# Order of the first query/key unit, and a passage into the feed-forward whose sums run on VectorE

## The chip, the cores and the metric

The kernel runs on one core of a Trainium2 chip. The metric is the device time of one execution in microseconds (us), read as the median of several executions.

## What is computed

One layer of a hybrid encoder, on 1024 tokens of width 1024 in float32. The input is RMS-normalised and projected; half of the heads do differential attention, the other half an mLSTM; both go through one output projection, then a gated feed-forward (SwiGLU) of hidden width 2816 and a last RMS norm follow. Cut to what matters here:

```
h = rms_norm(x, mix_norm_g);  z = h @ w_in
da_q, da_k, da_v, ml_q, ml_k, ml_v, ml_o, ml_i, ml_f = split(z)
x = x + concat(diff_attention(...), mlstm(...)) @ w_out
h2 = rms_norm(x, ffn_norm_g)
x = x + (silu(h2 @ w_gate) * (h2 @ w_up)) @ w_down
return rms_norm(x, final_norm_g)
```

## The kernel before, in words

**Numbers.** Every float32 matrix product is three matmuls on a high and a low part: `split` (L106) casts a tile to its high part on ScalarE (L107) and subtracts for the low part on VectorE (L108), or on GpSimd if the call names it. `mul12` (L182) is twelve 128x128 by 128x512 matmuls (L186 to L188) into one PSUM bank.

**Units.** The query/key projection and the feed-forward's gate and up projections use a 2x2 block scheme with seven products. `unit` (L193) works on one block of weights (`st`, four 128x512 tiles a11, a12, a21, a22) and on seven prepared operands: b11, b21, b22 (blocks of the activations) and t1 to t4 (their sums and differences). Its steps are numbered 1 to 7, each one `mul12`, and a sequence gives their order. Steps 1 and 2 add into bank 0, 5 and 3 into bank 3, 7 and 4 into bank 2, 6 into bank 1. Step 1 copies bank 0 into `u2` (ScalarE, L212), and step 2 then adds its product into the same bank. After step 6, `u2` takes bank 1 (L220); after step 7, c22 = u2 + bank 2 + bank 3 (L224, L225), and step 4 then adds into bank 2 (c21, L231). `SEQ0` is (1, 2, 5, 6, 7, 4, 3) and `SEQ` is (1, 5, 6, 7, 2, 4, 3); `SEQ0` is used by the first query/key unit and by the two first feed-forward units, `SEQ` by all others. A unit's split weights go through a ring of five (later seven) tiles.

**The first stage.** Eight query/key units run one after the other (L655 on). While the first one runs, ScalarE still finishes the output gate of the mLSTM (tanh, L534), the split of t4, and the first tables. `late_start` puts four of the tanh and t4 behind the cast of the first unit's fourth step.

**The passage.** The output projection (`out_proj`, L1099) goes row block by row block (128 tokens); for each it adds the residual (L1149, called the x add below), squares on ScalarE (L1169), takes the root on GpSimd (L1170, L102), scales on VectorE (`h2`, L1173), and later transposes `h2` (`h2_out`, L1071). The last four rows are the second half of the tokens, in the order given by `SLICES`. For each of them `t_slices` (L1054) makes one slice of t1, t3 and b22, and `t_sums` (L1065) adds two sums into `hst`, from which t2 and t4 are made. Of this, GpSimd does the low parts and the sums of the first two slices (`TP` = 2), two of the four low parts of b21 (`B21` = 2), and the low parts of t4; VectorE the rest. After the last row of the output projection TensorE runs step 1 of both first feed-forward units, then the eight transposes of the last row's `h2` (`th2l`), then the other steps of the two units by turns.

**Order.** TensorE's order is written by hand in the first stage and in the passage. The order of the instructions on the other engines, and on TensorE during attention, comes from a list scheduler that has its own clock; `tc.issue_after(i)` holds an instruction in that order behind `i`. All engines but the DMA work in the order of their queues.

Of the kernel before, what the change touches and what calls it, by code (L numbers as in the profile page):

```python
# [34 lines left out]
TP = 2  # L35
B21 = 2
# [8 lines left out]
SEQ0 = (1, 2, 5, 6, 7, 4, 3)  # L45
SEQ_D = (1, 5, 2, 3, 6, 7, 4)
# [16 lines left out]
def block_kernel(ctx, tc, x, xT, pos, cols, gate_b, lam_in, w_vg, w_mo, w_qk, w_dv,  # L63
# [42 lines left out]
    def split(hi, lo, src, eng=None):  # L106
        last_cast[0] = act.copy(hi, src)  # L107
        last_cast[1] = (eng or dve).tensor_sub(lo, src, hi.bitcast(F32))  # L108

# [83 lines left out]
    def unit(st, h, seq, psg, ringc, tmp, done, low=None):  # L193
# [13 lines left out]
        u2 = c22 = c21 = None  # L207
        for step in seq:
# [8 lines left out]
            elif step == 6:  # L217
                dve.tensor_tensor(a21, a22, a11, op=ALU.subtract)
                mul12(bank(1), wsplit(a21), h["t2"], True)
                dve.tensor_add(u2, u2, bk[1])  # L220
            elif step == 7:
                mul12(bank(2), wsplit(a11), h["t3"], True)
                c22 = tmp("u3")
                dve.tensor_add(c22, u2, bk[2])  # L224
                dve.tensor_add(c22, c22, bk[3])  # L225
            elif step == 2:
                mul12(bk[0], wsplit(a12), h["b21"], False)
            elif step == 4:
                mul12(bk[2], wsplit(a22), h["t4"], False)
                c21 = tmp("c21")  # L230
                dve.tensor_add(c21, u2, bk[2])  # L231
                if low:
                    low((c21, c22))
            elif step == 3:
                dve.tensor_tensor(a21, a12, a21, op=ALU.subtract)
                mul12(bk[3], wsplit(a21), h["b22"], False)
                dve.tensor_add(u2, u2, bk[3])
# [150 lines left out]
    with ExitStack() as pa:  # L388
# [3 lines left out]
        with ExitStack() as pm:  # L392
# [262 lines left out]
            for n_, b in enumerate(UO):  # L655
# [4 lines left out]
                u_ = q_unit(b, st, SEQ if n_ else SEQ0)  # L660
# [393 lines left out]
    def t_slices(c):  # L1054
        cs = slice(c * P, (c + 1) * P)
        p1, p2 = b12[:, :, cs], b22[:, :, cs]
        tt = bw.tile([P, 4, P], F32, tag="tt", name="tt", bufs=1)
        dve.tensor_sub(tt, p1, hst[0][:, :, cs])
        eng = pool if c in SLICES[:TP] else dve
        split(H["t1"][0][:, :, cs], H["t1"][1][:, :, cs], tt, eng)  # L1060
        dve.tensor_sub(p1, p2, p1)
        split(H["t3"][0][:, :, cs], H["t3"][1][:, :, cs], p1, eng)
        split(H["b22"][0][:, :, cs], H["b22"][1][:, :, cs], p2, eng)

    def t_sums(c):  # L1065
        cs = slice(c * P, (c + 1) * P)
        eng = pool if c in SLICES[:TP] else dve
        eng.tensor_tensor(hst[0][:, :, cs], hst[0][:, :, cs], b12[:, :, cs], op=ALU.add)
        eng.tensor_tensor(hst[1][:, :, cs], hst[1][:, :, cs], hst[0][:, :, cs], op=ALU.subtract)

    def h2_out(i, h2, ps_tile, gs=(0, 1)):  # L1071
# [16 lines left out]
        if i >= 4 and 1 in gs:  # L1088
            if hst:
                t_slices(i - 4)  # L1090
# [5 lines left out]

    n_wo = []

    def out_proj():  # L1099
# [29 lines left out]
        while True:  # L1129
# [5 lines left out]
            for u in range(2):  # L1135
# [4 lines left out]
                for n_, k in enumerate((4, 5, 6, 7, 0, 1, 2, 3)):  # L1140
# [9 lines left out]
                    if prev and 8 * u + n_ in th[2:]:  # L1150
                        g = th[2:].index(8 * u + n_)
                        h2_out(*prev, d_tile, (g,))
                        if g:
                            prev = None
                            if i == LAST:
                                t_sums(SLICES[2])
                    yield
                if u == 0 and i == LAST:
                    for n, g in (("b11", 0), ("b21", 1)):
                        H[n] = [slots.tile([P, 4, 512], F32R, tag=f"A{hl}{g}", name=n) for hl in range(2)]  # L1160
                        for q in range(4):
                            split(H[n][0][:, q], H[n][1][:, q], hst[g][:, q], pool if g and q < B21 else dve)
                    for c in SLICES[:2]:
                        t_sums(c)
            ssq = bw.tile([P, 1], F32, tag="ssq2", name="ssq2")
            sp.dma_start(x1_d[i], x1)
            with tc.high_priority():
# [5 lines left out]
                dve.tensor_scalar_mul(h2, x1, rs)  # L1173
            prev = (i, h2)
            if i == LAST:
                out_last.append(prev)
# [76 lines left out]
    two = [gu_unit(0, m, SEQ0) for m in range(2)]  # L1253
# [8 lines left out]
    for _ in range(2):  # L1262
        for u in two:
            next(u)
    t_sums(SLICES[3])
    for n, g in (("t2", 0), ("t4", 1)):
        H[n] = [slots.tile([P, 4, 512], F32R, tag=f"B{hl}{g}", name=n) for hl in range(2)]
        for q in range(4):
            split(H[n][0][:, q], H[n][1][:, q], hst[g][:, q], pool if g else dve)
# [13 lines left out]
    for _ in range(len(SEQ0)):  # L1283
        for u in two:
            next(u, None)
# [250 lines left out]
```

## Time and profile before

| what | value |
|---|---|
| median of 3 runs | 1218.44 us (1218.09 to 1219.29) |
| the profiled execution's own time | 1217.11 us |
| its span, first to last instruction | 1215.3 us |
| TensorE busy in the span | 1179.6 us (97%) |
| VectorE busy | 874.8 us (72%) |
| ScalarE busy | 526.3 us (43%) |
| GpSimd busy | 145.0 us (12%) |
| mean granted TensorE clock | 0.991 |

The profiled execution lies 1.3 us under the median of the runs, and 1.8 us of it lie outside its span. Engines: PE is TensorE, DVE VectorE, ACT ScalarE, POOL GpSimd, SP the queue that issues most DMAs.

### The profile page before, as it was taken

What the parts mean: (1) busy time and instruction counts of PE and PEld (TensorE: products, weight loads), DVE (VectorE), ACT (ScalarE), POOL (GpSimd) and SP (SyncE); (2) the same over time, 40 slices, a digit from 0 to 9 for tenths busy, and PEclk for the clock granted to TensorE, in tenths of its full rate; (3) what the DMA queues carried; (4) which work ended last, traced back from release to release, by engine and by line L of the source; (5) the groups of instructions that cost most, each with busy time, mean ns of one, the idle gap of its engine ahead of it and who ended that gap; (6) DMA issues with size and microseconds to landing.
All of it is one profiled execution on the core that took longest, in us unless ns stands there. A gap on an engine that the chain in (4) does not pass through costs nothing.

```text
span 1215.3 us, 15877 instructions
## 1 busy us (share of the span) xinstructions
PE 1179.6 (97%) x5692; PEld 973.4 (80%) x5692; DVE 874.8 (72%) x1520; ACT 526.3 (43%) x1111; POOL 145.0 (12%) x125
## 2 busy tenths in 40 slices
PE   9899999899989999998999999999999999999997
PEld 7678888898877888876888888888888888888885
DVE  8768899566768766659766766667666779765674
ACT  6723354335666555546333223332333245444552
POOL 0100000120101100043301110111101111000000
PEclk9999999999999999999999999999999999999999
DMA  9467743700667442150323230322223269733241
GB/s 332 167 170 192 219 128 123 258 19 19 215 224 229 149 139 95 57 221 18 113 87 130 95 130 36 130 109 117 79 87 130 96 242 352 259 99 112 79 149 70
DMA packets 87487, 172.37 MB, mean 142 GB/s; under 512 B 9968, under 2 KB 42864, under 8 KB 81008
## 3 DMA queue, kind: packets, MB, share of 16 engines
q1 hardware_dynamic: 85656, 169.73, 40.8%
q10 hardware_dynamic: 1752, 1.62, 0.4%
q8 instruction: 45, 0.74, 0.3%
q14 instruction: 34, 0.28, 0.1%
HBM read 117.58 MB, written 53.74 MB: 141 GB/s over the span
## 4 chain that ended last, share of the span: by engine, by line
PE 86%; DMA 2%; issue 2%; DVE 2%; ACT 2%; POOL 1%; SPq 0%; ACTq 0%; POOLq 0%; DVEq 0%
PE g L186 16%; PE g L187 16%; PE g L188 16%; PE y L1453 6%; PE y L1452 6%; PE y L1454 6%; PE dwo L1145 2%; PE dwo L1143 2%; PE dwo L1144 2%; PE to L333 2%; PE s L290 1%; PE s L291 1%; PE ddv L143 1%; PE ddv L142 1%; PE ddv L144 1%
## 5 line engine op out<-in xcount | busy, mean ns | idle before, releaser
L107 ACT CAST w<-st 128x512 fp32r<-128x512 f32 x218 | 133.4, 620 | 292.6 <-PE g L188 158.1
L108 DVE TENSOR_TENSOR w<-st,w 128x512 fp32r<-128x512 f32 x218 | 159.2, 733 | 91.7 <-ACT w L107 90.3
L186 PE MATMUL g<-t,w 128*128 128x512 f32 x448 | 177.9, 397 | 0.0
L187 PE MATMUL g<-t,w 128*128 128x512 f32 x448 | 177.1, 395 | 0.0
L188 PE MATMUL g<-t,w 128*128 128x512 f32 x448 | 176.4, 394 | 0.0
L1453 PE MATMUL y<-fhl,w 128*128 128x512 f32 x308 | 122.1, 397 | 0.0
L1452 PE MATMUL y<-fhl,w 128*128 128x512 f32 x308 | 121.8, 395 | 0.0
L1454 PE MATMUL y<-fhl,w 128*128 128x512 f32 x308 | 120.9, 393 | 0.0
L187 PE MATMUL g<-b,w 128*128 128x512 f32 x264 | 104.9, 397 | 0.0
L186 PE MATMUL g<-b,w 128*128 128x512 f32 x264 | 104.2, 395 | 0.0
L188 PE MATMUL g<-b,w 128*128 128x512 f32 x264 | 104.0, 394 | 0.0
L186 PEld LDWEIGHTS g<-t,w 128*128 128x128 f32 x448 | 84.2, 188 | 22.4 <-DVE u L224 2.6
L188 PEld LDWEIGHTS g<-t,w 128*128 128x128 f32 x448 | 84.2, 188 | 20.1
L187 PEld LDWEIGHTS g<-t,w 128*128 128x128 f32 x448 | 84.3, 188 | 19.0
L107 ACT CAST w<-gs 128x512 fp32r<-128x512 f32 x76 | 46.5, 619 | 68.7 <-PE y L1454 51.6
L108 DVE TENSOR_TENSOR w<-gs,w 128x512 fp32r<-128x512 f32 x76 | 52.9, 703 | 28.8 <-ACT w L107 28.8
L108 DVE TENSOR_TENSOR fhl<-w,fhl 128x512 fp32r<-128x512 f32 x77 | 51.9, 710 | 26.2 <-ACT fhl L107 26.2
L1452 PEld LDWEIGHTS y<-fhl,w 128*128 128x128 f32 x308 | 57.8, 188 | 14.2
L1454 PEld LDWEIGHTS y<-fhl,w 128*128 128x128 f32 x308 | 57.9, 188 | 13.8
L1453 PEld LDWEIGHTS y<-fhl,w 128*128 128x128 f32 x308 | 58.0, 188 | 13.1
L107 ACT CAST fhl<-w 128x512 fp32r<-128x512 f32 x77 | 44.2, 618 | 46.7 <-PE y L1454 43.3
L1237 POOL TENSOR_TENSOR ss<-sg 128x512 f32<-128x512 f32 x11 | 17.3, 1569 | 354.2 <-DVE sg L1235 317.9
(342 smaller groups left out, 2539.2 us busy)
## 6 DMA issues: line engine op xcount, KB each, us to landing
st<-in_w_gu SPq DMA_DIRECT2D x22, 1024.0 KB
gs<-gm_d SPq DMA_DIRECT2D x76, 256.0 KB
gm_d<-sg SPq DMA_DIRECT2D x11, 1024.0 KB
w<-in_w_dn SPq DMA_DIRECT2D x44, 256.0 KB
gm_d<-ss SPq DMA_DIRECT2D x11, 768.0 KB
st<-in_w_qk SPq DMA_DIRECT2D x8, 1024.0 KB
qbuf<-q_d SPq DMA_DIRECT2D x64, 128.0 KB
q_d<-xt SPq DMA_DIRECT2D x24, 256.0 KB
```

Of the source, the lines that this page charges most:

```text
L107: last_cast[0] = act.copy(hi, src)
L108: last_cast[1] = (eng or dve).tensor_sub(lo, src, hi.bitcast(F32))
L186: pe.matmul(ps, w[0][:, ks], h[0][:, k, :], start=first and k == 0, stop=False, **sk)
L187: pe.matmul(ps, w[0][:, ks], h[1][:, k, :], start=False, stop=False, **sk)
L188: pe.matmul(ps, w[1][:, ks], h[0][:, k, :], start=False, stop=k == 3, **sk)
L333: pe.matmul(po[:, 0, :], at[:, j, :], dv[j // 4][:, j % 4, hh * P:(hh + 1) * P], start=(j == 0), stop=(j == i))
L1143: pe.matmul(ps, mh, wh, start=(n_ == 0), stop=False)
L1144: pe.matmul(ps, mh, wl, start=False, stop=False)
L1145: pe.matmul(ps, ml, wh, start=False, stop=(n_ == KC - 1))
L1452: pe.matmul(bk[q][b], gh, w[0], start=first and k == 0, stop=False, **sk)
L1453: pe.matmul(bk[q][b], gh, w[1], start=False, stop=False, **sk)
L1454: pe.matmul(bk[q][b], gl, w[0], start=False, stop=k == FH - 1, **sk)
```

## The change

Three things are changed. The first query/key unit takes the sequence of the others. The two first feed-forward units take a new sequence `SEQ1` = (1, 2, 5, 7, 6, 4, 3), in which step 7 comes before step 6, so `unit` computes c22 behind whichever of the two comes last. And in the passage all low parts and sums that GpSimd made are VectorE's now; the sums of all four slices, and the third part (b22) of the last two, are made later: held in the scheduler's order behind the low part of t3 of the last slice, as t3 of the third slice and the later steps of the two units are held behind the scaling of the last row (`scaled`).

```diff
-TP = 2
-B21 = 2
+SEQ1 = (1, 2, 5, 7, 6, 4, 3)
...
+        def c22_of():
+            nonlocal c22
+            c22 = tmp("u3")
+            dve.tensor_add(c22, u2, bk[2])
+            dve.tensor_add(c22, c22, bk[3])
...
                 dve.tensor_add(u2, u2, bk[1])
+                if 2 in bk:
+                    c22_of()
             elif step == 7:
                 mul12(bank(2), wsplit(a11), h["t3"], True)
-                c22 = tmp("u3")
-                dve.tensor_add(c22, u2, bk[2])
-                dve.tensor_add(c22, c22, bk[3])
+                if 1 in bk:
+                    c22_of()
...
-                u_ = q_unit(b, st, SEQ if n_ else SEQ0)
+                u_ = q_unit(b, st, SEQ)
...
-    def t_slices(c):
+    def t_slices(c, parts=(0, 1, 2)):
...
-        eng = pool if c in SLICES[:TP] else dve
-        split(H["t1"][0][:, :, cs], H["t1"][1][:, :, cs], tt, eng)
-        dve.tensor_sub(p1, p2, p1)
-        split(H["t3"][0][:, :, cs], H["t3"][1][:, :, cs], p1, eng)
-        split(H["b22"][0][:, :, cs], H["b22"][1][:, :, cs], p2, eng)
+        if 0 in parts:
+            tt = bw.tile([P, 4, P], F32, tag="tt", name="tt", bufs=1)
+            dve.tensor_sub(tt, p1, hst[0][:, :, cs])
+            split(H["t1"][0][:, :, cs], H["t1"][1][:, :, cs], tt)
+        if 1 in parts:
+            dve.tensor_sub(p1, p2, p1)
+            t3_in[0] = split(H["t3"][0][:, :, cs], H["t3"][1][:, :, cs], p1)
+        if 2 in parts:
+            split(H["b22"][0][:, :, cs], H["b22"][1][:, :, cs], p2)
...
-        eng = pool if c in SLICES[:TP] else dve
-        eng.tensor_tensor(hst[0][:, :, cs], hst[0][:, :, cs], b12[:, :, cs], op=ALU.add)
-        eng.tensor_tensor(hst[1][:, :, cs], hst[1][:, :, cs], hst[0][:, :, cs], op=ALU.subtract)
+        dve.tensor_add(hst[0][:, :, cs], hst[0][:, :, cs], b12[:, :, cs])
+        dve.tensor_sub(hst[1][:, :, cs], hst[1][:, :, cs], hst[0][:, :, cs])
...
-                t_slices(i - 4)
+                t_slices(i - 4, {SLICES[2]: (0,), SLICES[3]: (0, 1)}.get(i - 4, (0, 1, 2)))
...
-                            split(H[n][0][:, q], H[n][1][:, q], hst[g][:, q], pool if g and q < B21 else dve)
-                    for c in SLICES[:2]:
-                        t_sums(c)
+                            split(H[n][0][:, q], H[n][1][:, q], hst[g][:, q])
...
-                dve.tensor_scalar_mul(h2, x1, rs)
+                scaled[0] = dve.tensor_scalar_mul(h2, x1, rs)
...
+                with tc.issue_after(scaled[0].ins):
+                    t_slices(SLICES[2], (1,))
...
-    two = [gu_unit(0, m, SEQ0) for m in range(2)]
+    two = [gu_unit(0, m, SEQ1) for m in range(2)]
...
-    for _ in range(2):
+    for n in range(3):
         for u in two:
-            next(u)
-    t_sums(SLICES[3])
+            with tc.issue_after(scaled[0].ins) if n == 2 else ExitStack():
+                next(u)
+    for c in SLICES:
+        with tc.issue_after(t3_in[0].ins):
+            t_sums(c)
...
-            split(H[n][0][:, q], H[n][1][:, q], hst[g][:, q], pool if g else dve)
+            split(H[n][0][:, q], H[n][1][:, q], hst[g][:, q])
+        if g == 0:
+            for c in SLICES[2:]:
+                with tc.issue_after(t3_in[0].ins):
+                    t_slices(c, (2,))
```

How the order moves, at three places. TensorE, at the end of step 1 of the first query/key unit (`g_575` is its bank 0; `hT_126`, `hT_127` are b11, `hT_128`, `hT_129` b21, `t_531`, `t_532` t1), before:

```order
L187 MATMUL g_575<-hT_127,w 128x512
L188 MATMUL g_575<-hT_126,w 128x512
L186 MATMUL g_575<-hT_128,w 128x512
L187 MATMUL g_575<-hT_129,w 128x512
L188 MATMUL g_575<-hT_128,w 128x512
```

and in the change:

```order
L187 MATMUL g_575<-hT_127,w 128x512
L188 MATMUL g_575<-hT_126,w 128x512
L186 MATMUL g_595<-t_531,w 128x512
L187 MATMUL g_595<-t_532,w 128x512
L188 MATMUL g_595<-t_531,w 128x512
```

The second product no longer goes into bank 0: step 5 follows step 1, and b21 comes as the fifth product. ScalarE's queue at that place in the change (`og` is the gate's tanh, `t4x` the high part of t4, `u_591` the copy of bank 0):

```order
L106 CAST w<-st 128x512 x3
L542 ACTIVATE og<-po_166,rstdh 128x512
L106 CAST w<-st 128x512
L542 ACTIVATE og<-po_167,rstdh 128x512
L542 ACTIVATE og<-po_168,rstdh 128x512
L542 ACTIVATE og<-po_169,rstdh 128x512
L106 CAST t4x_647<-xx 128x512 x4
L648 ACTIVATE an<-an 128x2
L106 CAST w<-st 128x512
L219 COPY u_591<-g_575 128x512
```

The copy keeps its place at the end; one weight cast more (three here, two before) stands ahead of the gate. VectorE in the passage, around the last row's scaling (`h_5613` before, `h_5602` in the change; `x_5411` is the row's output), before:

```order
L1068 TENSOR_TENSOR hst_5256<-hst_5256,h2r_3670 128x4x128
L1149 TENSOR_TENSOR x_5411<-dwo,x_5411 128x512
L108 TENSOR_TENSOR t_5250<-h2r_3670,t_5249 128x4x128
L108 TENSOR_TENSOR w<-st,w 128x512
L1069 TENSOR_TENSOR hst_5258<-hst_5258,hst_5256 128x4x128
L218 TENSOR_TENSOR st<-st 128x512
L1173 TENSOR_SCALAR h_5613<-x_5411,rs 128x1024
```

and in the change:

```order
L1159 TENSOR_TENSOR x_5411<-dwo,x_5411 128x512
L107 TENSOR_TENSOR w<-st,w 128x512
L107 TENSOR_TENSOR t_5248<-tt,t_5247 128x4x128
L1179 TENSOR_SCALAR h_5602<-x_5411,rs 128x1024
L1070 TENSOR_TENSOR h2r_3670<-h2r_3671,h2r_3670 128x4x128
L225 TENSOR_TENSOR st<-st 128x512
L107 TENSOR_TENSOR w<-st,w 128x512
```

No sum stands ahead of the scaling any more, and two instructions instead of four stand between the x add and the scaling. GpSimd's queue in the passage keeps only the small instructions of the root; before, this stood ahead of the last of them:

```order
L108 TENSOR_TENSOR b_5552<-hst_5258,b_5551 128x512 x2
L1068 TENSOR_TENSOR hst_5256<-hst_5256,h2r_3670 128x4x128 x2
L1069 TENSOR_TENSOR hst_5258<-hst_5258,hst_5256 128x4x128 x2
L1170 TENSOR_SCALAR ssq_5611<-ssq_5611 128x1
L102 TENSOR_TENSOR rs<-ssq_5611,mhalf 128x1
L108 TENSOR_TENSOR t_5774<-hst_5258,t_5773 128x512 x4
```

The three rows of sums and low parts ahead of the root, and the four low parts of t4 behind it, are gone from that queue.

## Rows read from the trace of the kernel before

**Rows 1.** Page, part 1: busy time, share of span, instructions of each engine.
```profile
PE 1179.6 (97%) x5692; PEld 973.4 (80%) x5692; DVE 874.8 (72%) x1520; ACT 526.3 (43%) x1111; POOL 145.0 (12%) x125
```

**Rows 2.** PE's waits, whole span: line, releaser, total us, times, longest.
```profile
PE th2l L1075 <- DVE h L1173: 5.3, 1, 5.3
PE to L333 <- ACT at L326: 5.1, 6, 2.6
...
PE dvg L142 <- DVE u L237: 2.2, 1, 2.2
...
PE g L186 <- DVE uq L224: 0.8, 1, 0.8
```

**Rows 3.** Timeline of PE, first unit: start, us, instruction, [idle before <- releaser].
```profile
50.73 0.40 PE L186 MATMUL g<-hT,w 128*128 128x512 f32 x1
...
58.63 0.80 PE L186 MATMUL g<-hT,w 128*128 128x512 f32 x1 [4.95 <-ACT u L212]
...
78.27 0.39 PE L186 MATMUL g<-hT,w 128*128 128x512 f32 x1
```

**Rows 4.** Windows: us, busy (instructions) of PE, PEld, DVE, ACT, POOL, clock, DMA.
```profile
58.60:62.60 4.00, 3.97 (x9) 3.14 (x10) 0.60 (x2) 0.00 (x0) 0.00 (x0) 0.50 0.74 311
62.60:72.00 9.40, 9.22 (x40) 7.14 (x38) 5.45 (x12) 1.96 (x4) 0.00 (x0) 1.00 0.46 131
...
700.00:900.00 200.00, 200.00 (x860) 160.94 (x859) 135.09 (x184) 60.29 (x103) 29.14 (x20) 1.00 0.28 104
```

**Rows 5.** Timeline of ACT around the copy of the first unit's bank 0.
```profile
55.30 2.18 ACT L107 CAST t4x<-xx 128x512 fp32r<-128x512 f32 x4
...
57.98 0.60 ACT L212 COPY u<-g 128x512 f32<-128x512 f32 x1
```

**Rows 6.** Timeline of PE in the passage.
```profile
546.74 0.63 PE L1075 MATMUL td<-ident,h 128*128 128x128 f32 x4 [1.12 <-DVE h L1173]
547.13 0.48 PE L1143 MATMUL dwo<-wo,w 128*128 128x512 f32 x1
...
553.69 0.39 PE L1145 MATMUL dwo<-wo,w 128*128 128x512 f32 x1
...
564.97 1.97 PE L1075 MATMUL th2l<-ident,h 128*128 128x128 f32 x8 [5.31 <-DVE h L1173]
...
568.15 0.39 PE L187 MATMUL g<-b,w 128*128 128x512 f32 x1
```

**Rows 7.** Timeline of POOL in the passage.
```profile
544.68 3.05 POOL L108 TENSOR_TENSOR b<-hst,b 128x512 fp32r<-128x512 f32 x2
553.77 5.79 POOL L1068 TENSOR_TENSOR hst<-hst,h2r 128x512 f32<-128x512 f32 x2 [6.04 <-DVE b L108]
559.52 3.38 POOL L1069 TENSOR_TENSOR hst<-hst,hst 128x512 f32<-128x512 f32 x2
...
563.59 0.54 POOL L102 TENSOR_TENSOR rs<-ssq,mhalf 128x1 f32<-128x1 f32 x1
```

**Rows 8.** Timeline of DVE in the passage.
```profile
528.41 0.68 DVE L1149 TENSOR_TENSOR x<-dwo,x 128x512 f32<-128x512 f32 x1
531.28 0.75 DVE L1173 TENSOR_SCALAR h<-x,rs 128x1024 f32<-128x1024 f32 x1 [2.18 <-POOL rs L102]
...
544.82 1.78 DVE L1173 TENSOR_SCALAR h<-x,rs 128x1024 f32<-128x1024 f32 x1
...
556.62 0.68 DVE L1149 TENSOR_TENSOR x<-dwo,x 128x512 f32<-128x512 f32 x1
...
561.71 1.74 DVE L218 TENSOR_TENSOR st<-st 128x512 f32<-128x512 f32 x1
...
566.16 0.68 DVE L1081 TENSOR_TENSOR h2r<-th2l,colt 128x512 f32<-128x512 f32 x1
...
572.78 0.69 DVE L235 TENSOR_TENSOR st<-st 128x512 f32<-128x512 f32 x1
```

**Rows 9.** Windows: the passage as one stretch, columns as in rows 4.
```profile
553.00:571.00 18.00, 12.69 (x54) 10.29 (x53) 17.25 (x24) 8.16 (x18) 10.19 (x6) 0.91 0.07 29
```

More of the change, by code (lines that the diff above doesn't have):

```diff
@@ L108, in split @@
         last_cast[1] = (eng or dve).tensor_sub(lo, src, hi.bitcast(F32))
+        return last_cast[1]
     def split_scaled(hi, lo, src, scale):
@@ L1052, in block_kernel @@
     H, hst, late_c, td_pool = {}, [], [], [psd]
-    def t_slices(c):
+    def t_slices(c, parts=(0, 1, 2)):
         cs = slice(c * P, (c + 1) * P)
         p1, p2 = b12[:, :, cs], b22[:, :, cs]
-        tt = bw.tile([P, 4, P], F32, tag="tt", name="tt", bufs=1)
-        dve.tensor_sub(tt, p1, hst[0][:, :, cs])
-        eng = pool if c in SLICES[:TP] else dve
-        split(H["t1"][0][:, :, cs], H["t1"][1][:, :, cs], tt, eng)
-        dve.tensor_sub(p1, p2, p1)
-        split(H["t3"][0][:, :, cs], H["t3"][1][:, :, cs], p1, eng)
-        split(H["b22"][0][:, :, cs], H["b22"][1][:, :, cs], p2, eng)
+        if 0 in parts:
[7 more added lines that the diff above has]
+            split(H["b22"][0][:, :, cs], H["b22"][1][:, :, cs], p2)
     def t_sums(c):
         cs = slice(c * P, (c + 1) * P)
-        eng = pool if c in SLICES[:TP] else dve
-        eng.tensor_tensor(hst[0][:, :, cs], hst[0][:, :, cs], b12[:, :, cs], op=ALU.add)
-        eng.tensor_tensor(hst[1][:, :, cs], hst[1][:, :, cs], hst[0][:, :, cs], op=ALU.subtract)
+        dve.tensor_add(hst[0][:, :, cs], hst[0][:, :, cs], b12[:, :, cs])
+        dve.tensor_sub(hst[1][:, :, cs], hst[1][:, :, cs], hst[0][:, :, cs])
     def h2_out(i, h2, ps_tile, gs=(0, 1)):
@@ L1095, in d_tile @@
         return td_pool[0].tile([P, 4, P], F32, tag="d", name="td")
+    scaled, t3_in = [None], [None]
     n_wo = []
@@ L1154, in out_proj @@
                             prev = None
-                            if i == LAST:
-                                t_sums(SLICES[2])
                     yield
@@ L1282, in block_kernel @@
     raw_tiles(ssp, "12", "x12", 8, 3)
-    for _ in range(len(SEQ0)):
+    for _ in range(len(SEQ1)):
         for u in two:
-            next(u, None)
+            with tc.issue_after(scaled[0].ins):
+                next(u, None)
     for j in range(1, FH):
```

## The prediction

> **What bounds the kernel now.** I read the busy times first [rows 1]: TensorE is busy 97% of the span, VectorE 72%, GpSimd 12%. Two later views tell what that 97% is made of. In a stretch where TensorE is never idle and the granted clock is 1.00, its 860 matmuls take 200 us, 0.2326 us each [rows 4]: one of the seven steps of a unit (12 matmuls) takes 2.79 us, a unit of 84 takes 19.5. No edit of this change touches the number of matmuls, so the only time to be had is where TensorE waits or goes slower than that. The list of its waits [rows 2] names the places: 5.3 us at the last row's transposes (`th2l`), 5.1 in six waits in attention (largest 2.6), 2.2 at one wait in the first value projection (`dvg`), 0.8 for `uq`. The largest wait of the first stage is seen in the timeline: 4.95 us for the copy of bank 0 [rows 3]. Of these the change aims at the copy, `uq` and `th2l`.
>
> **First unit, what it loses now.** It begins at 50.73 and the next one at 78.27 [rows 3]: 27.5 us, against 19.5 for 84 matmuls at full pace, so 8.0 us are lost. They can be named. 4.95 is the idle time: step 2 adds into bank 0, which ScalarE copies only at 57.98 to 58.58, behind the four casts of t4 of 55.30 to 57.48 [rows 5]. Behind that idle time the granted clock is 0.50, the 1.2 GHz level, and nine matmuls take 4.0 us where the 40 behind them go at 0.235 each (9.40 by 40) at 1.00 [rows 4]: 4.0 less 9 by 0.235 is 1.9. The wait for `uq` ahead of step 4 is 0.8 [rows 2]. 0.35 is left over.
>
> **First unit, in the change.** Steps 5, 6 and 7 stand between step 1 and step 2, so TensorE asks for the copied bank at 50.73 + 4 by 2.79 = 61.9. ScalarE's queue has one more weight cast ahead of the copy (three ahead of the gate instead of two); priced by a cast of t4, a quarter of 2.18 [rows 5], that is 0.55, and the copy ends near 59.1: 2.8 us to spare, where TensorE was 4.95 late. Step 4 then asks for `c22` at 64.7. That needs step 7's bank (ready at 61.9) and two additions of about 0.6, so 63.1: step 2, which stands between them now, covers it with 1.6 to spare. b21, which step 2 reads, is only asked for later than before. t1 to t3, which are asked for earlier, are made ahead of the unit's start; their lateness would be the one thing to cost here, at most what is gained. With no idle time there is no reason for the lower clock. I take the whole **8.0**; bounds 0 (something else is late by as much) and 8.0.
>
> **Passage, what it loses now.** `th2l` waits 5.31 [rows 6]. After it, from 564.97 to 568.15, eight transposes and three matmuls take 3.18. Four transposes took 0.39 at 546.74 [rows 6], so the normal time is 2 by 0.39 + 3 by 0.2326 = 1.5; **1.7** is the slow restart. And 1.12 is the wait for the row before it (`td` at 546.74). Together 5.31 + 1.7 + 1.1 = 8.1; I take **8.0**.
> Where it comes from: the last output matmul starts at 553.69 [rows 6] and the x add that reads its bank starts at 556.62 [rows 8], 2.5 us behind its end: VectorE is in other work. From there to the scaling takes until about 564.2, because the root's last instruction runs at 563.59 [rows 7], behind four sums that kept GpSimd from 553.77 to 562.90. Undisturbed, the same chain takes 2.87 us from x add to scaling (528.41 to 531.28) and 0.75 for the scaling [rows 8]. The earlier wait has the same source: the scaling took 1.78 at 544.82 [rows 8] instead of 0.75, while GpSimd ran two low parts from 544.68 to 547.73 [rows 7].
>
> **Passage, in the change.** All times here are on the clock of the trace of before, so ahead of the 8.0 of the first stage. Without the 1.1 the last output matmul ends at 553.69 + 0.39 - 1.1 = 553.0. The x add starts by 553.3; 2.87 to the scaling, plus up to 0.6 for casts ahead of the square on ScalarE, plus 0.75: `h` is there at 556.9 to 557.6. TensorE gets to the transposes after step 1 of both units, at 564.97 - 5.31 - 1.1 = 558.6. So this wait ends, with about 1 us in hand; and without idle time the slow restart goes.
>
> **What takes its place.** VectorE gets 16 more instructions: six low parts of slices, two of b21, four sums, four low parts of t4. At normal pace VectorE does 11 of this size in 6.62 us (566.16 to 572.78 [rows 8]), 0.60 each, so **9.6 us** of work move onto an engine that was busy 17.25 of 18.0 us here [rows 9]. Against that, part of its busy time was only slowness beside GpSimd: a 128x512 subtraction took 1.74 at 561.71 while GpSimd was in its sums, against 0.68 to 0.69 [rows 8]. What matters is the first thing TensorE will be kept from. In the queue's order I count 41 VectorE instructions from the end of the scaling to the `c22` of the first of the two units, which step 4 must wait for, because it adds into the bank that `c22` reads. 557.6 + 41 by 0.60 + 0.7 for the last one's end = 582.9, if none of them waits. TensorE, after eight transposes (0.8) at 558.6, wants that step after eight steps (step 5, 7, 6 and 2 of both units): 558.6 + 0.8 + 8 by 2.79 = 581.7. So I expect a **new wait of about 1.0 us** for `c22`; bounds 0 and 3 (one more pause for t2 or a weight cast, and the slow restart behind it). The operands ahead of it are on time by the same count: t1 at 563.8 (wanted 565.0), t3 at 564.4 (wanted 570.6), t2's first part at 572.3 (wanted 576.1). GpSimd keeps the root's four small instructions alone. The weights' transfers into `st` go out when `a11` to `a22` are last read; those reads shift with TensorE, and no TensorE wait in [rows 2] is on a transfer here.
>
> **Attention.** The scheduler's clock sees other costs, and shuffles some instructions of all engines in and behind attention: the transposes of the first row stand somewhat later, the first output matmuls four places earlier. I price this at 0, with 1.5 to either side, about half of the largest wait there (2.6 [rows 2]).
>
> **Sum.** -8.0 - 8.0 + 1.0 = -15.0. The profiled execution's own time is 1217.1, so 1202.1; the median of the runs lies 1.3 above it, so **1203.5 us**.
>
> **The rivals.**
> *VectorE becomes the bound in the passage.* It is the engine with the least room there [rows 9], and takes 9.6 us more. If all of it shows (every wait of TensorE goes to VectorE's queue as soon as the root is out of the way), the sum is -16.0 + 9.6 = -6.4 and the time 1212.0. Against it: the operands' dates above, and the 1.7 us instructions that become 0.6. The Trainium skill (Perfetto Trace Analysis, Optimizing Scalar/DVE Operations) speaks against this change: with VectorE saturated, moving work to ScalarE or GpSimd may make sense. The change does the reverse; by that sentence the time would be this rival's. The same section adds that both share a port into SBUF, so that moving between those two might not help; the 1.74 beside 0.69 agrees with that part. Chance 0.15.
> *The first stage's gain is eaten later.* Units 1 to 7 and the value projection come 8 us earlier; if their weights or VectorE's rotation of q and k are already just in time, the wait at `dvg` (2.2 [rows 2]) grows by what was won. Then only the passage counts: 1218.4 - 7.0 = 1211.4. For it: `dvg` waits on VectorE already. Against: behind the first unit VectorE is busy 5.45 of 9.40 us and the DMA share is 0.46 [rows 4]. Chance 0.09.
> *Nothing comes of it*: the copy is still late, and step 1 of the passage still waits as long for another operand. Within 2.4 us of 1218.4; chance 0.05.
> *Slower.* VectorE's long instructions in the passage are not GpSimd's doing, but come with the pieces that they read. Then the pace stays near the mean of 0.60 and 1.78, 1.19 each, and 41 instructions to `c22` take 24 us longer than reckoned. Without the first 1.2 to 2 us of slack that is +25 - 16 + some 1 of restart, about 1228. The point from which it decides: 16 us by 41, a pace of 0.98 instead of 0.60. For it: the 17.25 of 18.0 for 24 instructions [rows 9], 0.72 each even as a mean. Against: the 11 in a row at 0.60 lie in the same passage [rows 8], and the 1.78 and 1.74 both fall on a time when GpSimd was busy [rows 7]. Chance 0.04.
>
> **How the numbers follow.** My forecast, with its neighbourhood (1199 to 1208: attention's 1.5 both ways, the new wait 0 to 3, a unit's operand 1 to 2 late), has 0.62; another 0.05 lies below 1199, where attention's waits go as well. The range has to take in the two middle rivals: 1199.0 to 1212.5. What can be told from no change here is 0.2%, 2.4 us. Faster by more: 0.62 + 0.05 + 0.15 + 0.09 = 0.91; the same 0.05; slower 0.04.
>
> **What will show it.** In the first unit: no wait at the second product into bank 0, granted clock 1.00 all through, the second unit starting near 70.3. In the passage: no wait at `th2l`, the scaling at most 4 us behind the x add, GpSimd all but idle, VectorE in a row at 0.60 each, and the only wait of TensorE above half a microsecond for `c22` at step 4 of the first unit. I am wrong if VectorE's instructions stay long without GpSimd, if `t1`'s slices keep TensorE waiting behind the transposes, or if the 8 us are gone by the start of attention.

## The result and the profile after

The changed kernel takes 1204.78 us (median of 4 runs, 1201.22 to 1206.66) against 1218.87 beside it: ratio 0.9882, 95% interval 0.9858 to 0.9905. That is 14.1 us; 15.0 were forecast. The profiled execution took 1204.77 us, its span is 1203.0, so it can be set against the 1217.11 and 1215.3 of before.

The page's busy times answer to [rows 1], and the list of TensorE's waits, over the whole span, to [rows 2]:

```profile
PE 1177.0 (98%) x5692; PEld 970.0 (81%) x5692; DVE 875.6 (73%) x1536; ACT 526.8 (44%) x1111; POOL 118.9 (10%) x109
```

```profile
PE to L341 <- ACT at L334: 6.9, 9, 2.6
PE dvg L142 <- DVE u L245: 2.4, 1, 2.4
PE g L186 <- DVE u L212: 1.2, 2, 0.9
```

The waits for the copy, for `uq` and for `th2l` are gone. VectorE has 16 instructions more (1536 against 1520) and all but the same busy time, 875.6 against 874.8 us: the 9.6 us that it took over are paid by instructions that no longer run at 1.7 us beside GpSimd. New are two waits for `c22` (1.2 us in all), and the waits for `at` in attention have grown from 5.1 in 6 to 6.9 in 9.

The timeline of TensorE of the changed kernel, at the places that matter (start, duration, instruction, idle time before and its releaser):

```profile
51.23 0.40 PE L186 MATMUL g<-hT,w 128*128 128x512 f32 x1
...
70.74 0.39 PE L186 MATMUL g<-hT,w 128*128 128x512 f32 x1
...
350.39 0.40 PE L144 MATMUL ddv<-w,hT 128*128 128x512 f32 x1
...
388.62 0.60 PE L1135 MATMUL td<-ident,mt 128*128 128x128 f32 x4
...
553.49 1.04 PE L1084 MATMUL th2l<-ident,h 128*128 128x128 f32 x8
...
555.28 0.40 PE L187 MATMUL g<-b,w 128*128 128x512 f32 x1
...
577.17 0.47 PE L186 MATMUL g<-t,w 128*128 128x512 f32 x1 [0.35 <-DVE u L212]
...
603.38 0.50 PE L186 MATMUL g<-t,w 128*128 128x512 f32 x1 [0.89 <-DVE u L212]
...
1195.68 0.40 PE L1470 MATMUL y<-fhl,w 128*128 128x512 f32 x1
```

Three rows of the kernel before that belong to them and are not among [rows 3] and [rows 6]:

```profile
357.86 0.40 PE L144 MATMUL ddv<-w,hT 128*128 128x512 f32 x1
...
393.83 0.60 PE L1125 MATMUL td<-ident,mt 128*128 128x128 f32 x4
...
1206.75 0.40 PE L1454 MATMUL y<-fhl,w 128*128 128x512 f32 x1
```

Put beside the same instruction in the trace of before, these give an account by stage. A shift is the start after less the start before; where no pair of rows is shown it is the median over the matmuls of 10 us.

| up to | before | after | shift | this stage |
|---|---|---|---|---|
| start of the first unit | 50.73 | 51.23 | +0.50 | +0.5 (ahead of the change) |
| start of the second unit | 78.27 | 70.74 | -7.53 | **-8.03** |
| last matmul of the last value projection | 357.86 | 350.39 | -7.47 | +0.1 |
| a `td` group in attention | 393.83 | 388.62 | -5.21 | **+2.26** |
| ahead of the passage, near 540 | | | -4.97 | +0.24 |
| second matmul group behind `th2l` | 568.15 | 555.28 | -12.87 | **-7.90** |
| behind step 4 of the two first units, near 595 | | | -12.25 | **+0.6** |
| behind step 4 of the next unit, near 620 | | | -11.09 | **+1.15** |
| last matmul | 1206.75 | 1195.68 | -11.07 | 0 |

Another 1.2 us of the 12.3 lie behind the last matmul, in the last stores: no instruction differs there. They are no gain of the change. From the start of the last matmul to the end of the span it is 8.5 us in this trace of before, and 7.3 to 7.6 in the traces of the changed kernel and of all twelve versions below.

Windows over the first unit and the passage (columns as in [rows 4]):

```profile
51.20:70.80 19.60, 19.60 (x86) 15.84 (x85) 16.34 (x32) 11.19 (x21) 0.00 (x0) 1.00 0.66 216
550.00:556.00 6.00, 6.00 (x32) 4.98 (x31) 4.97 (x9) 4.31 (x12) 0.73 (x2) 1.00 0.19 77
556.00:576.00 20.00, 20.00 (x88) 16.16 (x87) 19.81 (x34) 11.82 (x20) 0.00 (x0) 1.00 0.00 1
```

TensorE has no idle time in any of the three, and the granted clock is 1.00 where it was 0.50 behind the copy [rows 4] and 0.91 in the passage [rows 9]. The first unit takes 70.74 less 51.23, 19.51 us; 84 by 0.2326 was the forecast. ScalarE's queue there is as reckoned, the copy still behind t4 and ending at 59.61, while TensorE asks for it at 62.37:

```profile
56.33 2.19 ACT L106 CAST t4x<-xx 128x512 fp32r<-128x512 f32 x4
...
59.01 0.60 ACT L219 COPY u<-g 128x512 f32<-128x512 f32 x1
```

VectorE and GpSimd in the passage, the x add, the root and the scaling of the last row, and what stands ahead of the first `c22` (L212):

```profile
548.33 0.68 DVE L1159 TENSOR_TENSOR x<-dwo,x 128x512 f32<-128x512 f32 x1
...
551.24 0.76 DVE L1179 TENSOR_SCALAR h<-x,rs 128x1024 f32<-128x1024 f32 x1 [1.03 <-POOL rs L101]
...
575.75 0.68 DVE L107 TENSOR_TENSOR w<-st,w 128x512 fp32r<-128x512 f32 x1
576.35 0.67 DVE L212 TENSOR_TENSOR u<-u,g 128x512 f32<-128x512 f32 x1
```

```profile
550.39 0.19 POOL L1176 TENSOR_SCALAR ssq<-ssq 128x1 f32<-128x1 f32 x1 [10.66 <-ACT h L1175]
550.66 0.54 POOL L101 TENSOR_TENSOR rs<-ssq,mhalf 128x1 f32<-128x1 f32 x1
```

From x add to scaling it is 2.91 us (548.33 to 551.24); before, some 7.5 lay between them [rows 7, 8]. `h` is there at 552.0, 1.5 us ahead of the transposes. Behind it VectorE works almost without a pause: the 41st instruction, the first addition of `c22`, starts at 576.35, 40 steps of 0.61 us behind the first (551.91). TensorE comes to step 4 at 576.43 + 0.23 = 576.66 and gets its bank at 577.17, 0.51 late (the list has 0.35, since it counts from the modelled end of the matmul before).

### The profile page after: what moved, and what is told of

Same layout as the page of the kernel before. It is cut to its first block, busy times and chain, and to the rows that moved or that the text cites. A ratio compares the mean times of both kernels' runs of the same rounds, so it can differ in the third digit from the quotient of the medians.

```text
span 1203.0 us, 15867 instructions
## 1 busy us (share of the span) xinstructions
PE 1177.0 (98%) x5692; PEld 970.0 (81%) x5692; DVE 875.6 (73%) x1536; ACT 526.8 (44%) x1111; POOL 118.9 (10%) x109
## 4 chain that ended last, share of the span: by engine, by line
PE 87%; DVE 4%; DMA 3%; issue 2%; ACT 2%; SPq 1%; POOL 0%; ACTq 0%; POOLq 0%; DVEq 0%
PE g L186 15%; PE g L187 15%; PE g L188 15%; PE y L1469 6%; PE y L1468 6%; PE y L1470 6%; PE dwo L1153 2%; PE dwo L1154 2%; PE to L341 2%; PE dwo L1155 2%; PE s L298 1%; PE s L299 1%; PE po L144 1%; PE po L143 1%; PE po L142 1%
## 5 line engine op out<-in xcount | busy, mean ns | idle before, releaser
L186 PEld LDWEIGHTS g<-b,w 128*128 128x128 f32 x264 | 49.5, 188 | 12.1
```

Source lines behind the costliest of these rows:

```text
L186: pe.matmul(ps, w[0][:, ks], h[0][:, k, :], start=first and k == 0, stop=False, **sk)
```

## The experiments

All of them ask one of four things: do the two parts of the change stand for themselves, what in the passage frees the last row, what in attention costs 2.3 us, and can the new waits be had back. Ratios are to the kernel before on the same chip.

### One part alone

`e1` takes the first line of the diff alone, `e2` everything but that line.

```diff
-                u_ = q_unit(b, st, SEQ if n_ else SEQ0)
+                u_ = q_unit(b, st, SEQ)
```

> Only the first query/key unit gets the new sequence; the passage stays as before. By my account the first unit gives 8.0 us (second unit starts 8 us earlier, no wait for the copy), and the 2.3 us lost in attention between 360 and 385 us come from the same edit, because the scheduler's clock reaches attention earlier and sets another order there: time about 5.7 us under the kernel before, about 1213, and the new waits for the transposed probabilities (to) are there. Rival: attention's loss comes from the passage's edit (its instructions compete in the same scheduler); then this kernel gains the whole 8, about 1211.

> Only the passage is changed; the first unit keeps its old sequence. By my account attention is as before, the wait at the last row's transposes goes with the slow restart and the 1.1 us ahead (7.9 us), and 1.75 us come back as two waits for c22: 6 to 7 us under the kernel before, about 1212. Rival (attention's loss belongs to this edit): about 1214.5, with the new waits in attention here.

`e1`: 1210.03 us, 0.9931 (0.9905 to 0.9957). `e2`: 1209.8 us, 0.9931 (0.9907 to 0.9954). Both are faster than was expected (about 1213 and 1212), and the total of `e1` lies at its rival's 1211; so the expectations are decided by the traces, stage by stage, and not by the totals. The product of the two ratios is 0.986, the whole change 0.988: within the intervals the parts add. Of the waits of `e1`, the one at `th2l` is untouched, and the nine in attention are there:

```profile
PE to L333 <- ACT at L326: 6.9, 9, 2.6
PE th2l L1075 <- DVE h L1173: 5.3, 1, 5.3
```

In `e1` the second unit comes 8.0 us earlier, as in the changed kernel; `e2` keeps the old 5.0 us for the copy and gets the passage's -7.9, +0.6 and +1.15. The lists of the order say why the nine waits belong to `e1`: its TensorE order in attention is word for word that of the changed kernel, that of `e2` that of the kernel before. So the edit of the first unit makes the scheduler sort transposes and products in attention differently; that its own clock reaches attention at another time is the likely way, and is not shown. But `e2` lost 1.3 us in attention too, with the old order. That missed its expectation, and is taken up below.

### What frees the last row: the engine, or the place in the queue

`e3`, `e4` and `e5` leave the first unit as before. `e4` is the kernel before with VectorE in GpSimd's place and nothing held back:

```diff
-        eng = pool if c in SLICES[:TP] else dve
+        eng = dve
...
-                            split(H[n][0][:, q], H[n][1][:, q], hst[g][:, q], pool if g and q < B21 else dve)
+                            split(H[n][0][:, q], H[n][1][:, q], hst[g][:, q])
```

`e3` is `e2` with GpSimd's share of before put back, and `e5` is `e3` with its sums held behind the root (the first line of the cut is `e3`'s):

```diff
+        eng = pool if c in SLICES[:2] else dve
...
-                rsqrt_of(rs, ssq)
+                rooted[0] = rsqrt_of(rs, ssq)
...
-        with tc.issue_after(t3_in[0].ins):
+        with tc.issue_after(t3_in[0].ins), tc.issue_after(rooted[0].ins):
             t_sums(c)
```

> The passage's new order (sums and later slices held behind the scaling, step 7 before step 6) with GpSimd doing what it did before; first unit as before. If what delayed the last row's scaling was the place of the sums in GpSimd's queue, the order alone removes most of it: the scaling comes within 1 us of its time in the changed kernel and th2l waits under 1 us; GpSimd's slow sums then come later and put other waits (t2 or t4 late, each GpSimd instruction 1.7 to 2.9 us where VectorE needs 0.6): 1212 to 1218. Rival: the engine counts, since VectorE is slowed by whatever GpSimd does in the passage; then th2l still waits 2 us or more.

> All of GpSimd's sums and low parts in the passage on VectorE, but nothing held behind the scaling and the old sequence of steps; first unit as before. If the engine is what counts, th2l's wait nearly goes (under 1 us): about 1212. If the place behind the scaling counts too, VectorE's queue has up to eight more instructions of 0.6 us ahead of the x add or the scaling, and th2l still waits 1 to 4 us: 1213 to 1216.

> As the run before with GpSimd kept (first unit as before), but GpSimd's four sums now really stand behind the root's last instruction in its queue. If the sums' place in GpSimd's queue was the whole cause, the last row's scaling comes 3.5 to 4 us behind the x add and th2l waits under 0.5 us, as in the changed kernel; what remains is the 1.1 us wait one row earlier (GpSimd's two low parts beside the scaling), and afterwards the sums on GpSimd make t2 late by 0 to 4 us: 1210 to 1215. Rival: the engine counts by itself; then th2l still waits 1.5 us or more although no sum stands ahead of the root.

`e3`: 1213.17 us, 0.9966 (0.995 to 0.9982). It did not test what it was meant to. A hold binds instructions of the holder's engine alone, and the holder is VectorE's; so the four sums still stood ahead of the root on GpSimd:

```profile
553.05 3.98 POOL L1079 TENSOR_TENSOR hst<-hst,h2r 128x512 f32<-128x512 f32 x2 [6.04 <-DVE b L107]
556.99 2.52 POOL L1080 TENSOR_TENSOR hst<-hst,hst 128x512 f32<-128x512 f32 x2
559.59 0.19 POOL L1178 TENSOR_SCALAR ssq<-ssq 128x1 f32<-128x1 f32 x1
```

`th2l` waited 2.3 us, which decides neither for the expectation nor for its rival. It is less than 5.3 since VectorE, relieved of its own sums, stood idle beside them for the greater part, and GpSimd's took 2.0 and 1.3 us (means of two) instead of 2.9 and 1.7 [rows 7].

`e4`: 1214.04 us, 0.9965 (0.9953 to 0.9977), `th2l` waits 3.5 us. The sums are VectorE's and the root has GpSimd for itself, but two things hold it up. VectorE's sums stand ahead of the x add, which comes at 555.33, and then this (the row before stands above it):

```profile
543.44 0.53 POOL L1170 TENSOR_SCALAR ssq<-ssq 128x1 f32<-128x1 f32 x1 [11.78 <-ACT h L1169]
...
557.33 3.55 POOL L1170 TENSOR_SCALAR ssq<-ssq 128x1 f32<-128x1 f32 x1 [12.40 <-ACT h L1169]
560.96 0.54 POOL L102 TENSOR_TENSOR rs<-ssq,mhalf 128x1 f32<-128x1 f32 x1
```

One instruction on 128x1 takes 3.55 us on GpSimd, where the same took 0.19 in the changed kernel. VectorE's queue is without a gap from 540.2 to 560.8 in `e4`; in the changed kernel it has a pause just there (1.03 ahead of 551.24). So VectorE can hold back GpSimd, not only the other way round. A full queue alone does not do it: at 543.44, inside the same stretch without a gap, the instruction took 0.53, and in none of the other traces does it take more than 0.55 near the passage. What decides between the two is not shown.

`e5`: 1214.47 us, 0.9976 (0.9965 to 0.9986). Here the place is right and the engine is not. The root is through at 557.35, TensorE waits for nothing at `th2l`, and the passage has given 6.8 us by then, where the changed kernel has 7.9. The missing 1.1 us are the wait one row earlier: it is there in `e3` and `e5`, whose two low parts of b21 are GpSimd's, and gone in `e2` and `e4`. Then most of it is lost again, since the sums now run beside the scaling and what follows it. VectorE and GpSimd of `e5`:

```profile
557.39 1.77 DVE L1181 TENSOR_SCALAR h<-x,rs 128x1024 f32<-128x1024 f32 x1 [1.57 <-POOL rs L101]
559.08 1.76 DVE L1071 TENSOR_TENSOR h2r<-h2r,h2r 128x512 f32<-128x512 f32 x1
560.76 1.79 DVE L225 TENSOR_TENSOR st<-st 128x512 f32<-128x512 f32 x1
562.48 1.78 DVE L107 TENSOR_TENSOR w<-st,w 128x512 fp32r<-128x512 f32 x1
564.19 0.68 DVE L107 TENSOR_TENSOR t<-h2r,t 128x512 fp32r<-128x512 f32 x1
```

```profile
557.32 2.97 POOL L1079 TENSOR_TENSOR hst<-hst,h2r 128x512 f32<-128x512 f32 x2
...
560.25 3.46 POOL L1080 TENSOR_TENSOR hst<-hst,hst 128x512 f32<-128x512 f32 x2
```

Four of VectorE's instructions take 1.77 us beside four of GpSimd's at 1.3 to 1.75; the next one, alone again, 0.68. TensorE then waits for t1:

```profile
567.98 0.50 PE L186 MATMUL g<-t,w 128*128 128x512 f32 x1 [2.08 <-ACT t L106]
```

Behind this wait the granted clock is 0.50 from 570.0 to 573.4, and of the 6.8 us only 2.3 are left. That decides between the theories: the place in the queue removes the wait at `th2l`, and the engine is what keeps the gain. Near 620 the passage has given 2.5 us in `e3`, 2.8 in `e4` and 1.6 in `e5`; with both halves of the edit, in `e2`, it has given 6.1 (7.9 less 1.75). The Trainium skill (SBUF — State Buffer, SBUF: two separate sides) says that VectorE and GpSimd share a port pair, which whichever starts first holds for its whole instruction while the other fully blocks; of VectorE's instructions it names those with two inputs in SBUF (against a GpSimd instruction that reads SBUF) or in a two-port mode. The rows of `e5` agree: the two alternate at one pace of 1.7 us.

### The copy's place in the first unit

`e8` leaves the old sequence and holds the last four tanh and t4 behind the copy:

```diff
-                    late_start(last_cast[0])
+                    late_start(u2_in[0])
```

> The kernel before with its old sequence in the first unit, but the last four tanh of the gate and the casts of t4 are held behind the copy of bank 0 in ScalarE's queue. If the copy's place in that queue was the cause of the 4.95 us, the copy runs at about 53.6 to 54.3, TensorE waits 0.5 to 1.0 us for it, the granted clock stays at 1.00, and the second unit starts 5 to 7 us earlier than before. The scheduler sets another order in attention, so the total is not to be read, only the first stage. Rival: the wait only moves to the next thing ScalarE owes (t4, or the fourth step's weights), and the unit gains less than 3 us.

ScalarE of `e8`, and TensorE at the second product:

```profile
55.06 0.58 ACT L212 COPY u<-g 128x512 f32<-128x512 f32 x1
55.54 2.43 ACT L534 ACTIVATE og<-po,rstdh 128x512 f32<-128x512 f32 x4
```

```profile
55.69 0.50 PE L186 MATMUL g<-hT,w 128*128 128x512 f32 x1 [1.25 <-ACT u L212]
```

The copy comes a little later than expected and TensorE still waits 1.25 us for it, but the granted clock stays at 1.00, and the second unit starts some 5.5 us earlier (shift -4.74, of which +0.77 came in ahead). So ScalarE's queue was the cause. The new sequence gives 8.0 because it lets TensorE work on something else meanwhile, and covers `uq` as well, for which `e8` still waits 0.9. In all 1209.38 us, 0.993 (0.9915 to 0.9945).

### What attention lost

`e7` is the changed kernel with one more sequence for the first unit, with which TensorE has in attention the very order of the kernel before. `e9` is `e6` (below) with two buffers for the rows `mt`, which are scaled and then stored; `e11` is both.

```diff
-                u_ = q_unit(b, st, SEQ)
+                u_ = q_unit(b, st, SEQ if n_ else (1, 5, 6, 7, 4, 2, 3))
```

```diff
-            mt = mw.tile([P, 2, P], F32, tag="maskb", name="mt0")
+            mt = mw.tile([P, 2, P], F32, tag="mt01", name="mt0", bufs=2)
... (mt1 alike)
```

> The changed kernel with the first unit's sequence 1, 5, 6, 7, 4, 2, 3: step 4 directly behind step 7, so that TensorE waits for c22 in the first unit (1 to 2 us lost of its 8.0), but the scheduler's order in attention is that of the kernel before. If attention's loss of 2.1 to 2.3 us is due to that order, the waits for the transposed probabilities between 360 and 385 us are back to those of before and the whole stands within 1 us of the changed kernel. Rival: the loss is due to the earlier start of attention itself (operands from memory or other engines late by the same amount); then it stays and this kernel is 1 to 2 us slower than the changed one.

> The run e6 (the changed kernel with the first gate's sums on VectorE), and two buffers instead of one for the normalised attention rows (mt) that are stored to memory. In attention VectorE stood 2.2 us at one instruction until the store of the row before had landed. If that wait is the second part of attention's loss (beside the order), VectorE no longer waits for a store there, TensorE's waits for ct and c between 360 and 385 us get smaller, and the time falls by 0.5 to 2 us against e6, to about 1201. Rival: the whole loss is in the order of the transposes and products; then no more than 0.3 us.

> The run e9 with the first unit's sequence of e7, so that attention has the order of the kernel before: about 1 us lost in the first unit for c22, and 1 to 2 us back in attention by the order: between 1 us faster and 0.5 us slower than e9. If the order alone makes the loss, attention's lead over the kernel before stays whole between 360 and 390 us here (within 0.5), which it did not in e7 (1.0 lost).

`e7`: 1203.0 us, 0.9881 (0.9866 to 0.9895). `e9`: 1201.83 us, 0.9855 (0.984 to 0.987). `e11`: 1202.49 us, 0.9865 (0.9849 to 0.9882). In time they can't be told apart. `e7`'s waits for `at` are back to 5.1 in 6, as expected, but 1.5 us for `ct` have come up beside them, as in `e2`. So the order is a part of the cause and not the whole. The traces tell the parts. The table has the stretch of attention from the last value-projection matmul to the `td` group of the account (350.39 to 388.62 in the changed kernel), one execution for each number. In `e9`, `e10` and `e11` two output matmuls stand behind that group and not ahead of it; 0.47 us are added for them, so that all numbers hold the same work.

| order in attention | one buffer for `mt` | two |
|---|---|---|
| of before | 36.0 (before), 37.2 (`e2`), 36.4 (`e3`), 35.8 (`e4`), 36.3 (`e5`), 36.6 (`e7`) | 36.4 (`e11`) |
| of the change | 38.2 (changed), 37.6 (`e1`), 39.2 (`e6`) | 37.7 (`e9`), 37.9 (`e10`) |

By the means the order costs about 1.4 us in the right column and some 2.0 in the left; in one cell the executions lie up to 1.6 apart. Most of it can be seen: all five traces with the new order have three waits for `at`, of 0.52, 0.46 and 0.57 us (1.55 together), that none with the old order has. A new order need not cost: that of `e8` is a third one, and there the shift goes from -7.5 to -8.9 between the last value projection and 540.

What is left, the loss of `e2`, is a store. VectorE of `e2` and what TensorE waits for, with the old order:

```profile
376.08 0.48 DVE L994 TENSOR_SCALAR mt<-ct,ff 128x128 f32<-128x128 f32 x2 [2.61 <-DMA mx_db<-mt]
```

```profile
376.91 0.46 PE L341 MATMUL to<-dv,at 128*128 128x128 f32 x2 [1.68 <-DVE ct L344]
```

`mt` has one buffer, so the next row's scaling waits until the last row's store has landed, and the copy that frees TensorE's bank stands behind it in VectorE's queue. SyncE's queue in `e2` and in `e9`, where that store is issued:

```profile
367.80 0.42 SPq L1002 DMA_DIRECT2D mx_db<-mt  x1
```

```profile
358.37 0.41 SPq L1002 DMA_DIRECT2D mx_db<-mt  x1
```

It is issued at 367.80 and released VectorE at 376.1, 8.3 us later, while the loads of q and k fill the queues (DMA share 0.92 from 370 to 380). In the kernel before it was issued 1.2 us later, at 368.96, and VectorE went on at 375.8; VectorE stood 0.95 us at this instruction and nobody waited for it. In `e9` two of the three such waits that `e6` has are gone, and the stretch is 1.5 shorter; the third is left, because two buffers are used up by the two half rows in turn. `e11` has it too, and TensorE waits 1.5 us behind it; so `e11` does not test a kernel without that wait, which `e12` below does. VectorE of `e9`:

```profile
366.02 0.48 DVE L1000 TENSOR_SCALAR mt<-ct,ff 128x128 f32<-128x128 f32 x2 [2.38 <-DMA mx_db<-mt]
```

### The new waits

`e6` gives VectorE the four sums of the first gate as well, which GpSimd does from 590.71 in the changed kernel; `e10` holds a low part that isn't urgent behind `c22` in `e9`.

```diff
-            pool.tensor_sub(ss[:, 1], sg[:, 0], sg[:, 1])
+            eng = dve if j == 0 else pool
+            eng.tensor_sub(ss[:, 1], sg[:, 0], sg[:, 1])
```

```diff
-                mul12(bk[3], wsplit(a21), h["b22"], False)
+                with tc.issue_after(c22_in[0].ins) if seq == SEQ1 else ExitStack():
+                    w_ = wsplit(a21)
+                mul12(bk[3], w_, h["b22"], False)
```

> The changed kernel, and the four sums behind the first feed-forward block (GpSimd in 591 to 597 us) on VectorE as well. If the second c22 wait (0.9 us and the slow restart, 1.15 together) comes from VectorE's instructions that take 1.7 us beside these, it goes: about 1 us under the changed kernel. Rival: VectorE's queue is simply too long there, four more instructions of 0.6 make the wait longer, by up to 2 us.

> The run e9, and in the two first feed-forward units the low part of step 3's weights is held behind the first addition of c22 in VectorE's queue. The wait of 0.35 us (0.6 with the slow restart) at step 4 goes, about 0.5 us, if an instruction that stands ahead of c22 without need is what makes it late. Rival: VectorE's queue as a whole is too long, and the weights of step 3 become late instead: 0 to 1 us slower than e9.

`e6`: 1202.19 us, 0.9872 (0.9857 to 0.9886). VectorE ahead of the second wait in the changed kernel:

```profile
591.00 1.78 DVE L243 TENSOR_TENSOR st<-st 128x512 f32<-128x512 f32 x1
593.53 2.66 DVE L107 TENSOR_TENSOR w<-st,w 128x512 fp32r<-128x512 f32 x2 [0.74 <-ACT w L106]
596.23 1.67 DVE L221 TENSOR_TENSOR st<-st 128x512 f32<-128x512 f32 x1
...
602.65 0.68 DVE L212 TENSOR_TENSOR u<-u,g 128x512 f32<-128x512 f32 x1
```

and in `e6`:

```profile
590.51 0.68 DVE L1246 TENSOR_TENSOR ss<-sg 128x512 f32<-128x512 f32 x1
...
598.63 0.69 DVE L212 TENSOR_TENSOR u<-u,g 128x512 f32<-128x512 f32 x1 [0.78 <-PE g L188]
```

Four more instructions, and `c22` is done earlier; the wait at 603.38 is gone and the shift stays where it was (-13.96 before and -13.34 behind the first wait, no second step). Its cause was GpSimd beside VectorE, as expected. `e10`: the first wait goes too. The shift is -11.54 ahead of that place and -11.52 behind it, where the changed kernel loses 0.6. The time, 1202.61 us, 0.9862 (0.9844 to 0.9879), doesn't show half a microsecond.

`e12` puts it together, with `mt`'s second half rows alone in two buffers:

> Everything that the traces so far showed to pay: the changed kernel, the first gate's sums on VectorE, step 3's weights behind c22 in the first two feed-forward units, the first unit with step 4 before step 2 (attention in nearly the order of before), and one buffer for each of mt's first half rows and two for its second ones, so that the store that took 7.6 us to land in e9 is no longer waited for. By the traces: e11 less 0.5 for the c22 wait and less 0 to 1 for the store, about 1201. Rival: the gains lie within what differs from run to run (e9 to e11 lay between 1201.8 and 1202.6 with intervals that overlap); then 1202 to 1203.

1201.25 us, 0.9863 (0.9835 to 0.9892). In its trace the waits are gone as meant: none for `c22` is left in the feed-forward, no scaling of `mt` waits for a store, and attention's stretch takes 35.6 us (counted as in the table), less than before the change. The profiled execution took 1198.35 us, but the runs reach 1203.07. The time is the expected one, but the interval holds the ratio of the changed kernel (0.9882), as the rival of the expectation has it: `e12` is not shown to be faster. Of the versions tried it has the lowest median; by the ratio to the kernel before on the same chip `e9` (0.9855) lies ahead of it.

## Why the prediction was right, step by step

**The first unit** was taken at 8.0 and measured 8.03. The idle time, the low clock behind it and the wait for `uq` all went, `e8` shows ScalarE's queue as the cause, and the cover reckoned for the copy (2.8 us) was 2.76 (59.61 to 62.37).

**The passage's gain** was taken at 8.0 and measured 7.9. The chain from x add to scaling came out at 2.91 us, the undisturbed one of [rows 8] at 2.87. `e3` and `e5`, which differ in the place of GpSimd's sums alone, show that the sums ahead of the root make a wait (2.3 us against none), as the prediction read it; the other 3 us of the 5.3 went already in `e3`, where VectorE is idle beside most of them. One term was misread: between 564.97 and 568.15 stand eight transposes and four matmuls, not three. In the changed kernel the same stretch takes 1.79 us (553.49 to 555.28), so the slow restart was 1.4 and not 1.7, and the sum 7.8.

**The price on VectorE.** The pace of 0.60 became 0.61, and the new wait of 1.0 us for `c22` was 0.51, at the instruction named; with the first matmul behind it, a little longer, it makes 0.6, and the granted clock stays at 1.00, so the slow restart of the prediction's upper bound did not come. The sum had counted the last instruction twice: 41 by 0.60 holds its own time, and 0.7 for its end was added. The rival of a bound VectorE (1212.0) failed for the reason given against it: the 1.7 us instructions were GpSimd's doing, and what VectorE gained by their end covered what it took over. `e5` shows this apart: VectorE's instructions take 1.77 us only beside GpSimd's. VectorE was busy 19.81 of 20.0 us from 556, and TensorE lost nothing until 0.7 us behind the end of that window. The Trainium skill (Perfetto Trace Analysis, Optimizing Scalar/DVE Operations) says that with VectorE saturated it may make sense to move work to ScalarE or even GpSimd; here the reverse paid. The Trainium skill's next sentence there, that GpSimd and VectorE share a port and that moving work between them might not help, is the one that these runs bear out.

**The other rivals.** The gain of the first unit was not eaten at `dvg`: the wait there went from 2.2 to 2.4 us and the shift stayed at -7.5. VectorE's instructions did not stay long without GpSimd, so the slower time did not come.

**What was missed** is 2.26 and 1.15 us. Against these stand 0.4 that the first `c22` wait cost less than forecast, and the 1.2 us in the last stores, which are chance. Another 0.9 went in small terms, 0.5 of it ahead of the first unit. So in the two traces 12.3 us came of the 15.0, and that the total came so near is partly luck. *Attention was priced at 0, with 1.5 to either side*: the term was mis-sized. The shuffle was seen, but no price was worked out of it. Attention cost 2.26 in this trace; with one buffer the stretch took 1.6 to 3.3 us more than before in the new order, and in the old one between 0.2 less and 1.3 more. *The second `c22` wait*, one unit later, was not looked for: the prediction stopped its count of VectorE's queue at step 4 of the first two units, and GpSimd's next four instructions stand just behind.

**What differs between executions.** In the last value-projection stage, which is the same in all these kernels, some 2 us between executions come from the `dvg` wait (1.3 to 2.5 us) and TensorE's clock behind it. The granted clock was 0.50 there, the 1.2 GHz level, in the traces of before, the changed kernel, `e1`, `e4`, `e7` and `e10`, and 1.00 in the other eight. Against before these eight come out of it 1.6 to 2.4 us earlier than they went in, the other five between 1.0 earlier and 0.3 later. The changed kernel and `e2` (columns as in [rows 4], the clock is the third from the end):

```profile
212.30:215.70 3.40, 3.31 (x15) 3.31 (x16) 3.38 (x6) 1.24 (x1) 2.18 (x3) 0.50 0.55 183
```

```profile
220.00:224.00 4.00, 3.98 (x32) 3.98 (x33) 3.98 (x5) 1.25 (x1) 2.18 (x3) 1.00 0.44 133
```

What stays open: why the wait and the clock there differ from one execution to the next, and why the changed kernel's runs are 5 us apart.

## What to carry to other kernels

Where two engines slow each other, price a moved instruction by its undisturbed duration and count what the others get back; and look at both the engine and the place in the queue, for here either alone gave less than half. A sequence that puts independent work between a producer and the step that waits for its copy was worth more here than an earlier copy (8.0 against 5.5 us). Any edit ahead of a stage that a scheduler sorts is an edit of that stage as well: list its order before and after, and give it a price.

## What was not expected of the hardware

- A 128x1 instruction on GpSimd took 3.55 us beside a VectorE queue without a gap, once, and 0.53 earlier in the same stretch (`e4`); in a pause of VectorE it took 0.19.
- VectorE and GpSimd side by side went at one pace, 1.7 us an instruction each (`e5`), where alone VectorE's take 0.68 (`e5`) and GpSimd's 1.3 (`e3`).
- A store of 128x256 to memory released its buffer 8.3 us after it was issued, with the DMA share at 0.92 (`e2`).
- Behind the same wait in the same stage the granted clock was 0.50 in six traces and 1.00 in eight.
